# The start of a feed-forward stage: two weight blocks interleaved, with their operands built in a written order

## The chip, the cores and the metric

The kernel runs on one core of a Trainium2 chip. The metric is the device time of one execution in microseconds (us), taken as the median of several executions. Its engines are TensorE (PE), VectorE (DVE), ScalarE (ACT), GpSimd (POOL) and SyncE (SP), whose queue issues most DMA transfers. Each engine takes its instructions in order.

## The reference

One layer of a decoder over 1040 positions of width 1024 (16 learned meta tokens and 1024 tokens), all in float32:

```python
u = rmsnorm(h, mix_norm)
proj = u @ w_in + b_in                      # attention, gated linear attention and gate inputs
mixed = sigmoid(gate_a) * (y_att @ w_proj_attn) + sigmoid(gate_b) * (y_gla @ w_proj_gla)
h = h + mixed @ w_out
u = rmsnorm(h, ffn_norm)
a, v = split(u @ w_up, 2)                   # 1024 x 5632; a and v are 2816 wide
h = h + (gelu(causal_dwconv3(a)) * v) @ w_down
return rmsnorm(h, final_norm)[:, 16:]
```

## The kernel before

Every float32 operand of a matmul is split into a high part, rounded for the fast matmul type (ScalarE, a cast), and a low part, the rest (VectorE, a subtraction); a product is then three matmuls, high by high, high by low and low by high (L949 to L951).

The stages follow each other: the input projection (names d_q, d_gk, d_g), attention and gated linear attention woven into the gate projections, the output projection `w_out` (d_wo), the feed-forward product with `w_up` (m) and with `w_down` (dn). The residual h is held transposed in `hT`: eight strips of 128 channels by two halves of the tokens, 514 columns each, the first two columns of the second half being a copy of the last two of the first.

The `w_up` product is done in 22 blocks of 256 output channels; even blocks give a, odd ones v. Each block uses the seven-product form of a 2 x 2 matrix product: A11 to A22 are quarters of the weights (128 output channels by four strips), B11 to B22 quarters of u (four strips by one half of the tokens). P1, P2, P3 and P4 use B11, B21, B22 and T4; P5, P6, P7 use T1, T2, T3. The T operands are sums of quarters of u, made once, and all eight operands stay in SBUF as high and low parts. The weight sums S1 to S4 are made for each block on GpSimd (`sum_make`), and `w_split` splits the weight quarter of a product into one of six tiles. A product of an even block is two groups of 12 matmuls (258 and 256 columns), one of an odd block 12 matmuls of 512.

Around the change, from the last strips of `w_out` to the third block: `wout` adds a strip of the output projection to `hT` and squares it, with the squares summed on GpSimd into `rs`; `norm2` turns these sums into 1/rms by a matmul with `ones_m`, a square root and a reciprocal over all columns; `turn_out` transposes one half of `hT` on TensorE and stores it to DRAM for the final residual; `u2` scales a strip by its gain and 1/rms; `op_split` makes the high and low part of an operand. For the second half of the tokens all this comes after the last strip of `w_out`. Of the sums for the T operands, T1 (L1076) and T2 (L1081) are subtracted on VectorE, T3 (L1080) and T4 (L1089) on GpSimd.

The order of the instructions on each engine isn't that of the text: a planner in the framework reorders them by estimated costs and by the order of the text where two are ready. Buffers of a pool with the same tag follow each other in one place, and a new one waits for the last use of the old. PSUM has eight banks, named by the tags mm (3), s (2), pt (1) and pv (2).

In the input projection `tsum` loads pairs of `w_down` strips, sums them on VectorE and stores the sums to DRAM (`tw`, `t_d`); it is called once before every chunk of several products. The rotary step of the attention inputs goes through one buffer, `rs`, filled by four small transfers that ScalarE's queue issues (L314).

Of the kernel before, what the change touches and what calls it, by code (L numbers as in the profile page):

```python
# [46 lines left out]
def hybrid_block(ctx, tc, x, meta, mix_norm, w_in, b_in, w_alpha, b_alpha, sinks, ghn,  # L47
# [376 lines left out]
    run("gk0", CH_ALL, evac_gq(gk, bcol[:, 7:8], 1.0, 0), tsum)  # L424
# [439 lines left out]
    def turn_out(hf, tag, pool_):  # L864
        ht = pool_.tile([P, 4, D], F32, tag=tag, name=f"ht{hf}")
        for j in range(4):
            for h in range(2):
                tp = bank("pv" if h else "pt", f"th{hf}_{j}_{h}")
                for k in range(4):
                    pe.transpose(tp[:, k * P:k * P + P], hT[:, h * 4 + k, hf, 2 + j * P:2 + j * P + P], ident)  # L870
                (dve.tensor_copy if h else act.copy)(ht[:, j, h * 512:h * 512 + 512], tp)
# [24 lines left out]
    FIRST, ORDER = ("P1", "P2", "P3", "P6", "P7", "P5", "P4"), ("P1", "P2", "P6", "P7", "P5", "P3", "P4")  # L896
    seq = [(b, pn) for b in range(NB) for pn in (ORDER if b else FIRST)]
# [410 lines left out]
```

## Time and profile before

| | us |
|---|---|
| median of 3 runs (1442.51 to 1447.55) | 1442.79 |
| the profiled execution, its device time | 1442.23 |
| its span | 1440.5 |
| TensorE busy in the span | 1374.3 |
| VectorE busy | 913.5 |
| ScalarE busy | 581.6 |
| GpSimd busy | 426.0 |

A matmul's busy time includes an end that overlaps the next one, so a TensorE that is busy all the time may still be running at its lower clock. Idle time of an engine matters only where the next work of TensorE waits for it.

### The profile page before, as it was taken

Reading aid. Unit: us, or ns where it says so; the run is one execution under the profiler, and the core shown is the slowest. Engines: PE = TensorE matmul, PEld = TensorE weight load, DVE = VectorE, ACT = ScalarE, POOL = GpSimd, SP = SyncE. Lnnn points to the kernel's source line nnn. Section 1 sums busy time; section 2 is a strip of 40 time slices with the busy share of each in tenths; the row PEclk is TensorE's granted clock in tenths of the full one; section 3 lists DMA queues with packets and bytes.
Section 4 is the critical chain, followed back from the end, with each engine's and each line's share of the span. In section 5 each row is a group of like instructions: output and inputs, shape, how many; then the busy total and the mean of one; then the engine's idle time right before and its main releaser. Section 6 shows DMA issues by size and latency. Waiting matters only on the chain.

```text
span 1440.5 us, 21775 instructions
## 1 busy us (share of the span) xinstructions
PE 1374.3 (95%) x8213; PEld 1247.5 (87%) x8213; DVE 913.5 (63%) x1478; ACT 581.6 (40%) x1143; POOL 426.0 (30%) x298
## 2 busy tenths in 40 slices
PE   6979999989999999999996899999999999999997
PEld 6979999878989989999875788999999888788886
DVE  6565212566778876443659877776667777665674
ACT  6313221544545555443443433333323333554452
POOL 0220110111122222223234465676567653100000
PEclk9999999999999999999997999999999999999999
DMA  7789711113222324554321133332332234976642
GB/s 216 220 256 308 234 49 51 59 51 75 80 77 73 82 74 138 173 156 132 132 88 58 45 103 103 111 109 82 110 110 87 83 110 175 354 261 195 194 152 117
DMA packets 160871, 190.23 MB, mean 132 GB/s; under 512 B 19082, under 2 KB 115142, under 8 KB 160758
## 3 DMA queue, kind: packets, MB, share of 16 engines
q1 hardware_dynamic: 157670, 180.25, 39.7%
q10 hardware_dynamic: 3088, 8.51, 1.9%
q8 instruction: 67, 1.10, 0.3%
q14 instruction: 46, 0.38, 0.1%
HBM read 133.33 MB, written 52.74 MB: 129 GB/s over the span
## 4 chain that ended last, share of the span: by engine, by line
PE 68%; DVE 7%; ACT 1%; issue 1%; DMA 1%; POOL 1%; SPq 0%; DVEq 0%; ACTq 0%; POOLq 0%
PE m L951 10%; PE m L949 10%; PE m L950 10%; PE dn L1233 5%; PE dn L1234 5%; PE dn L1232 5%; PE d_g L91 3%; PE d_g L92 3%; PE d_g L93 3%; PE d_wo L91 2%; PE d_wo L92 2%; PE d_wo L93 2%; PE d_pj L91 2%; PE d_pj L92 2%; PE d_pj L93 2%
## 5 line engine op out<-in xcount | busy, mean ns | idle before, releaser
L949 PE MATMUL m<-op_T,wq 128*128 128x258 f32 (+2 forms) x528 | 170.8, 326 | 8.3 <-ACT op_T L889 8.3
L950 PE MATMUL m<-op_T,wq 128*128 128x258 f32 (+2 forms) x528 | 171.0, 324 | 1.3 <-DVE op_T L890 1.1
L951 PE MATMUL m<-op_T,wq 128*128 128x258 f32 (+2 forms) x528 | 170.1, 323 | 1.3 <-DVE wq L938 1.3
L91 PE MATMUL d_g<-uh,hi_g 128*128 128x342 f32 x480 | 159.6, 332 | 2.5 <-PEq L568 2.4
L92 PE MATMUL d_g<-ul,hi_g 128*128 128x342 f32 x480 | 157.0, 327 | 3.0 <-issue 3.0
L93 PE MATMUL d_g<-uh,lo_g 128*128 128x342 f32 x480 | 157.0, 327 | 0.0
L951 PE MATMUL m<-op_B,wq 128*128 128x256 f32 (+2 forms) x396 | 127.3, 322 | 4.4 <-DVE wq L938 4.4
L949 PE MATMUL m<-op_B,wq 128*128 128x256 f32 (+2 forms) x396 | 127.6, 323 | 1.6 <-ACT op_B L889 1.2
L950 PE MATMUL m<-op_B,wq 128*128 128x256 f32 (+2 forms) x396 | 127.6, 322 | 1.1 <-DVE op_B L890 1.1
L937 ACT CAST wq<-S 128x512 fp32r<-128x512 f32 x88 | 54.4, 623 | 170.7 <-PE m L951 154.6
L949 PEld LDWEIGHTS m<-op_T,wq 128*128 128x128 f32 x528 | 101.4, 193 | 16.8 <-ACT op_T L889 8.8
L950 PEld LDWEIGHTS m<-op_T,wq 128*128 128x128 f32 x528 | 101.5, 192 | 10.3 <-DVE op_T L890 2.4
L951 PEld LDWEIGHTS m<-op_T,wq 128*128 128x128 f32 x528 | 101.5, 193 | 9.2 <-DVE wq L938 1.5
L91 PEld LDWEIGHTS d_g<-uh,hi_g 128*128 128x128 f32 x480 | 93.1, 194 | 6.5 <-ACT gev L398 3.0
L93 PEld LDWEIGHTS d_g<-uh,lo_g 128*128 128x128 f32 x480 | 93.0, 194 | 3.8 <-issue 3.6
L938 DVE TENSOR_TENSOR wq<-st,wq 128x512 fp32r<-128x512 f32 x66 | 77.2, 1171 | 28.1 <-ACT wq L937 28.1
L92 PEld LDWEIGHTS d_g<-ul,hi_g 128*128 128x128 f32 x480 | 93.2, 194 | 0.5 <-issue 0.4
L965 DVE TENSOR_TENSOR wk<-wk,m 128x512 f32<-128x512 f32 (+2 forms) x99 | 55.1, 566 | 49.4 <-PE m L951 48.2
L1019 POOL TENSOR_TENSOR wk<-wk 128x1024 f32<-128x1024 f32 x22 | 58.1, 2643 | 93.1 <-DVE wk L965 90.7
L951 PEld LDWEIGHTS m<-op_B,wq 128*128 128x128 f32 x396 | 75.3, 190 | 10.6 <-DVE wq L938 4.8
L950 PEld LDWEIGHTS m<-op_B,wq 128*128 128x128 f32 x396 | 75.2, 190 | 7.7 <-DVE op_B L890 1.9
L949 PEld LDWEIGHTS m<-op_B,wq 128*128 128x128 f32 x396 | 75.0, 190 | 7.8 <-ACT op_B L889 1.4
(312 smaller groups left out, 3702.2 us busy)
## 6 DMA issues: line engine op xcount, KB each, us to landing
st<-in_w_up_dram SPq DMA_DIRECT2D x22, 1024.0 KB, 7.1
stage<-g_d SPq DMA_DIRECT2D x77, 256.0 KB, 4.5
tw<-in_w_down_dram SPq DMA_DIRECT2D x11, 1024.0 KB, 8.8
t_d<-tw SPq DMA_DIRECT2D x11, 1024.0 KB, 5.2
stage<-t_d SPq DMA_DIRECT2D x44, 256.0 KB, 3.0
gate_d<-gev SPq DMA_DIRECT2D x60, 171.0 KB, 2.9
st_g<-in_w_in_dram SPq DMA_DIRECT2D x20, 512.0 KB, 4.8
g_d<-wk SPq DMA_DIRECT2D x11, 768.0 KB
```

Source lines behind the costliest of these rows:

```text
L91: pe.matmul(o[:, :n], hi[:, k, :], rh(k), start=(k == 0), stop=False)
L92: pe.matmul(o[:, :n], hi[:, k, :], rl(k), start=False, stop=False)
L93: pe.matmul(o[:, :n], lo[:, k, :], rh(k), start=False, stop=(k == nk - 1))
L938: dve.tensor_tensor(t[:, 1], src, f32(t[:, 0]), ALU.subtract)
L949: pe.matmul(o[:, :m], t[:, 0, k], bh[:, k, a:a + m], start=(k == 0), stop=False)
L950: pe.matmul(o[:, :m], t[:, 0, k], bl[:, k, a:a + m], start=False, stop=False)
L951: pe.matmul(o[:, :m], t[:, 1, k], bh[:, k, a:a + m], start=False, stop=(k == 3))
L965: dve.tensor_tensor(dv[:, w], sv[:, w], o[:, :m], ALU.add)
L1019: pool.tensor_tensor(v, v, wk[:, 1028 + f * 1024:2052 + f * 1024].rearrange("p (h n) -> p h n", h=2), ALU.mult)
L1232: pe.matmul(o, gh[:, ts], dh, start=first, stop=False)
L1233: pe.matmul(o, gh[:, ts], dl, start=False, stop=False)
L1234: pe.matmul(o, gl[:, ts], dh, start=False, stop=last_)
```

## The change

The first two blocks of the `w_up` product are interleaved, and the stretch from the seventh strip of `w_out` to the last product of the second block is put in the order of the text on TensorE, VectorE, ScalarE and GpSimd (`manual_schedule`); SP's queue is still planned. In detail:

- Both first weight blocks are loaded early into one tile (`st01`), and their sums S1 and S3, S2 and S4 are made on GpSimd partly during `w_out`, in place of the quarters (`sum_first`). P1 and P2 of both blocks come first, then P3, P5, P6, P7, P4 of the two in turn.
- The second half of the tokens is transposed strip by strip (`turn_strip`), six of the eight strips during `w_out`, with all copies out of PSUM on ScalarE.
- The 1/rms of the second half is made token-major: eight matmuls of one column give the mean squares with tokens on partitions, root and reciprocal are taken over four columns, and four diagonal matrices (`dg`) times ones spread the result over a PSUM bank (`bc`), which `u2` reads.
- All eight sums for the T operands are on VectorE, in pairs of strips (1028 columns).
- The scratch tile `wk` is no longer a tile of its own but the place of `hT`. The gating of the first pair of blocks is moved into the third block.
- One product of the input projection, gk0, no longer calls `tsum` (three calls); the calls that are left come three chunks later.

```diff
-    run("gk0", CH_ALL, evac_gq(gk, bcol[:, 7:8], 1.0, 0), tsum)
+    run("gk0", CH_ALL, evac_gq(gk, bcol[:, 7:8], 1.0, 0))
...
+    def turn_strip(ht, k, tag="pv"):
+        tp = bank(tag, f"th1_{k}")
+        for j in range(4):
+            pe.transpose(tp[:, j * P:j * P + P], hT[:, k, 1, 2 + j * P:2 + j * P + P], ident)
+        act.copy(ht[:, :, k * P:k * P + P], tp.rearrange("p (j n) -> p j n", j=4))
+        if k % 4 == 3:
+            c = k // 4 * 512
+            sp.dma_start(h_d[4:8, :, c:c + 512].rearrange("j p n -> p j n"), ht[:, :, c:c + 512])
...
-    def u2(k, hf):
-        hv = hT[:, k, hf]
-        dve.scalar_tensor_tensor(hv, hv, fcol[:, k:k + 1], rs[hf], ALU.mult, ALU.mult)
-
-    def op_split(nm, i, m, src, eng=None):
-        hv, lv = (t[:, i:i + m] for t in ops[nm])
-        act.copy(hv, src)
-        (eng or dve).tensor_tensor(lv, src, f32(hv), ALU.subtract)
+    def u2(k, hf, scale=None):
+        hv = hT[:, k, hf, 2 if hf else 0:]
+        dve.scalar_tensor_tensor(hv, hv, fcol[:, k:k + 1], scale if hf else rs[hf], ALU.mult, ALU.mult)
+    def op_hi(nm, i, m, src):
+        act.copy(ops[nm][0][:, i:i + m], src)
+    def op_lo(nm, i, m, src):
+        dve.tensor_tensor(ops[nm][1][:, i:i + m], src, f32(ops[nm][0][:, i:i + m]), ALU.subtract)
...
-    FIRST, ORDER = ("P1", "P2", "P3", "P6", "P7", "P5", "P4"), ("P1", "P2", "P6", "P7", "P5", "P3", "P4")
-    seq = [(b, pn) for b in range(NB) for pn in (ORDER if b else FIRST)]
+    FIRST, ORDER = ("P3", "P5", "P6", "P7", "P4"), ("P1", "P2", "P6", "P7", "P5", "P3", "P4")
+    seq = [(b, pn) for b in range(2) for pn in ("P1", "P2")] + [(b, pn) for pn in FIRST for b in range(2)]
+    seq += [(b, pn) for b in range(2, NB) for pn in ORDER]
...
+    EARLY = ["s", "mm", "pv", "mm", "s", "mm", "pv", "s", "mm", "mm", "pt", "s", "mm", "pv", "mm", "s", "pv", "pv",
+             "mm", "pt", "mm"]
     def next_bank(name):
+        if EARLY:
+            return bank(EARLY.pop(0), name)
...
+    def sum_first(b, half):
+        a11, a12, a21, a22 = (quarter(b, q) for q in ("A11", "A12", "A21", "A22"))
+        s1 = s1t[:, b]
+        if half == 0:
+            pool.tensor_tensor(s1, a21, a22, ALU.add)
+            pool.tensor_tensor(a21, a11, a21, ALU.subtract)
+        else:
+            pool.tensor_tensor(a11, s1, a11, ALU.subtract)
+            pool.tensor_tensor(a12, a12, a11, ALU.subtract)
+        sums[b] = {"S1": s1, "S2": a11, "S3": a21, "S4": a12}
...
+            if mid and out_:
+                mid()
...
+    st01 = big.tile([P, 2, KT, 2, P], F32, tag="B1", name="st01")
+    s1t = p2.tile([P, 2, 4, P], F32, tag="xt", bufs=1, name="s1t")
+    hts = []
+    for i in range(6):
         wout(i, take(f"wo{i}_1"), (2,))
         if i == 0:
             norm2(0)
             norm2(1)
         elif i == 1:
-            turn_out(0, "B0", big)
-            pool.tensor_copy(hT[:, :, 1, 0:2], hT[:, :, 0, HQ - 2:HQ])
-            pool.tensor_copy(rs[1][:, 0:2], rs[0][:, HQ - 2:HQ])
+            hts.append(big.tile([P, 4, D], F32, tag="B0", name="ht0"))
+            turn_out(hts[0])
             op_tile(("B11", "B21"), big, "A")
             st_load(0)
-        elif i < 6:
+            st_load(1)
...
+                op_hi(nm, k % 4, 1, hT[:, k:k + 1, 0])
+                op_lo(nm, k % 4, 1, hT[:, k:k + 1, 0])
+            if i > 2:
+                if i == 3:
+                    hts.append(big.tile([P, 4, D], F32, tag="B0", name="ht1"))
+                for k in ((0, 1), (2, 3), (4,))[i - 3]:
+                    turn_strip(hts[1], k)
+            if i > 3:
+                sum_first(i - 4, 0)
+    pool.tensor_copy(hT[:, :, 1, 0:2], hT[:, :, 0, HQ - 2:HQ])
+    with tc.manual_schedule(engines={mybir.EngineType.PE, mybir.EngineType.DVE, mybir.EngineType.Activation,
+                                     mybir.EngineType.Pool}):
+        wout(6, take("wo6_1"), (2,))
+        turn_strip(hts[1], 5)
+        w_split(0)
+        w_split(3)
+        w_last = take("wo7_1")
+        w_split(1)
+        w_split(2)
+        o = dense(w_last, lambda k: mh[k // 4][:, k % 4, 514:1026], lambda k: ml[k // 4][:, k % 4, 514:1026], KT, 512,
+                  "wo7_2")
+        turn_strip(hts[1], 6)
+        hv = hT[:, 7, 1, 2:]
+        dve.tensor_tensor(hv, hv, o, ALU.add)
+        sq = p2.tile([P, 512], F32, tag="sg0", bufs=2, name="sq_last")
+        act.activation(sq, hv, AF.Square)
+        for b in range(2):
+            sum_first(b, 1)
+        op_tile(("B22",), big, "C1")
+        op_tile(("T2",), big, "C2")
+        op_tile(("T1",), b2, "E")
+        w_split(4)
+        w_split(5)
+        pr = {0: product(0)}
+        nt = bank("pt", "nt")
+        for j in range(4):
+            pe.matmul(nt[:, j:j + 1], rs[1][:, 2 + j * P:2 + j * P + P], ones_m[:, 0:1], start=True, stop=False)
+            pe.matmul(nt[:, j:j + 1], sq[:, j * P:j * P + P], ones_m[:, 0:1], start=False, stop=True)
+        act.activation(rt4[:, 0], nt[:, 0:4], AF.Sqrt, bias=eps_c, scale=1.0)
+        dve.reciprocal(rt4[:, 1], rt4[:, 0])
+        dg = p2.tile([P, 4, P], F32, tag="sg1", bufs=2, name="dg")
+        for j in range(4):
+            if j % 2:
+                dve.tensor_scalar(dg[:, j], ident, rt4[:, 1, j:j + 1], None, ALU.mult)
+            else:
+                act.activation(dg[:, j], ident, AF.Identity, scale=rt4[:, 1, j:j + 1])
+        bc = bank("pt", "bc")
+        turn_strip(hts[1], 7)
+        def spread():
+            for j in range(4):
+                pe.matmul(bc[:, j * P:j * P + P], ones_f, dg[:, j], start=True, stop=True)
+        pr[1] = product(1, spread)
+        p1a = b2.tile([P, HQ], F32, tag="rs1", name="p1_0")
+        p1v = b2.tile([P, HQ], F32, tag="rs0", name="p1_1")
+        keep_prod(0, p1a, pr[0])
+        w_split(6)
+        pr[2] = product(2)
+        w_split(7)
+        p2.release()
+        fp = tc.alloc_tile_pool(name="fp", bufs=1, reuse_waits="tile")
+        aa0 = fp.tile([P, 2, HQ], F32, name="aa0")
+        vt = fp.tile([P, 4, 4, P], F32, tag="S", bufs=1, name="vt").rearrange("p a k n -> p (a k n)")
+        vt = vt[:, 0:1024].rearrange("p (a n) -> p a n", a=2)
+        st_load(2)
+        st_load(3)
+        keep_prod(1, p1v, pr[2])
+        pr[3] = product(3)
+        def lo22(k):
+            op_lo("B22", k - 4, 1, hT[:, k:k + 1, 1])
+        for k in range(4, 8):
+            u2(k, 1, bc)
+            op_hi("B22", k - 4, 1, hT[:, k:k + 1, 1])
+            if k > 4:
+                lo22(k - 1)
+        lo22(7)
+        pr[4] = product(4)
+        pr[5] = product(5)
+        wk = hT.rearrange("p k h n -> p (k h n)")
+        def madd(dst, src, prod, off):
+            for o, a, m in prod:
+                dve.tensor_tensor(dst[:, a - off:a - off + m], src[:, a - off:a - off + m], o[:, :m], ALU.add)
+        def half(k, hf):
+            return hT[:, k:k + 2, hf]
+        madd(aa0[:, 0], p1a, pr[1], 0)
+        for k in range(4):
+            u2(k, 1, bc)
+        for k in (0, 2):
+            dve.tensor_tensor(half(k, 0), half(k, 1), half(k, 0), ALU.subtract)
+            op_hi("T1", k, 2, half(k, 0))
+        w_split(8)
+        for k in (0, 2):
+            op_lo("T1", k, 2, half(k, 0))
+        madd(vt[:, 0], p1v, pr[3], 2)
+        pr[6] = product(6)
+        pr[7] = product(7)
+        keep_prod(0, aa0[:, 1], pr[4])
+        keep_prod(1, vt[:, 1], pr[5])
+        for k in (0, 2):
+            dve.tensor_tensor(half(k, 1), half(k + 4, 1), half(k, 1), ALU.subtract)
+        op_tile(("T3",), big, "B0")
+        for k in (0, 2):
+            dve.tensor_tensor(half(k + 4, 1), half(k + 4, 1), half(k, 0), ALU.subtract)
+            op_hi("T2", k, 2, half(k + 4, 1))
+        w_split(9)
+        for k in (0, 2):
+            op_lo("T2", k, 2, half(k + 4, 1))
+            op_hi("T3", k, 2, half(k, 1))
+        pr[8] = product(8)
+        pr[9] = product(9)
+        w_split(10)
+        w_split(11)
+        for k in (0, 2):
+            op_lo("T3", k, 2, half(k, 1))
+        w_split(12)
+        w_split(13)
+        op_tile(("T4",), big, "B1")
+        for k in (0, 2):
+            dve.tensor_tensor(half(k + 4, 0), half(k + 4, 0), half(k + 4, 1), ALU.subtract)
+            op_hi("T4", k, 2, half(k + 4, 0))
+        madd(p1a, p1a, pr[8], 0)
+        madd(p1v, p1v, pr[9], 2)
+        for k in (0, 2):
+            op_lo("T4", k, 2, half(k + 4, 0))
+        pr[10] = product(10)
+        pr[11] = product(11)
+        pr[12] = product(12)
+        ca, cv, cv0 = whole(0, 1), whole(1, 1), whole(1, 0)
+        act.copy(cv0[:, 0], vt[:, 0])
+        w_split(14)
+        madd(ca[:, 0], p1a, pr[10], 0)
+        madd(ca[:, 1], ca[:, 0], pr[6], 0)
+        madd(aa0[:, 1], aa0[:, 1], pr[6], 0)
+        w_split(15)
+        pr[13] = product(13)
+        madd(cv[:, 0], p1v, pr[11], 2)
+        madd(cv[:, 1], cv[:, 0], pr[7], 2)
+        madd(cv0[:, 1], vt[:, 1], pr[7], 2)
+        sum_make(2)
+        dve.tensor_tensor(aa0[:, 1], aa0[:, 1], p1a, ALU.add)
+        w_split(16)
+        conv(0, 0)
+        madd(ca[:, 0], ca[:, 0], pr[12], 0)
+        conv(0, 1)
+        w_split(17)
+        dve.tensor_tensor(cv0[:, 1], cv0[:, 1], p1v[:, 0:512], ALU.add)
+        madd(cv[:, 0], cv[:, 0], pr[13], 2)
...
-    for n in range(2, len(seq)):
+    for n in range(14, len(seq)):
...
-            if pn == ("P5" if b == 0 else "P3"):
+            if b == 2 and pos in (2, 3):
+                gated(0, pos - 2)
+            if pn == "P3":
...
-    tl = b2.tile([P, 7, D], F32, tag="H", name="tl")
+    tl = wk[:, 0:7 * D].rearrange("p (a n) -> p a n", a=7)
```

## Rows read from the trace of the kernel before

**Rows 1.** Page: busy us, share of the span, instructions of an engine.
```profile
PE 1374.3 (95%) x8213; PEld 1247.5 (87%) x8213; DVE 913.5 (63%) x1478; ACT 581.6 (40%) x1143; POOL 426.0 (30%) x298
```

**Rows 2.** Waits of TensorE: line, released by, us in total, times, longest.
```profile
PE m L949 <- ACT op_T L889: 8.3, 2, 5.4
PE d_gk L91 <- ACT rt L308: 7.4, 1, 7.4
PE m L951 <- DVE wq L938: 5.7, 2, 4.4
```

**Rows 3.** Windows: length; busy PE, PEld, DVE, ACT, POOL; granted clock; DMA share; GB/s.
```profile
744.60:821.00 76.40, 55.28 (x288) 46.41 (x287) 67.47 (x83) 31.52 (x51) 33.14 (x22) 0.82 0.20 69
821.00:861.00 40.00, 40.00 (x256) 36.29 (x255) 29.45 (x41) 14.29 (x22) 26.85 (x15) 1.00 0.30 99
```

**Rows 4.** Timeline of TensorE: start, length, line, operation, count, idle before.
```profile
707.14 2.25 PE L870 MATMUL th<-ident,hT 128*128 128x128 f32 x16
...
744.60 0.28 PE L949 MATMUL m<-op_B,wq 128*128 128x258 f32 x1
...
747.51 1.12 PE L858 MATMUL n<-rs,ones_m 128*128 128x512 f32 x2
...
820.91 0.28 PE L949 MATMUL m<-op_B,wq 128*128 128x258 f32 x1
...
860.65 0.28 PE L949 MATMUL m<-op_B,wq 128*128 128x258 f32 x1
```

**Rows 5.** Timeline of VectorE in the same stretch.
```profile
753.39 3.34 DVE L860 RECIPROCAL rs<-rs 128x512 f32<-128x512 f32 x1
...
766.27 2.07 DVE L885 SCALAR_TENSOR_TENSOR hT<-hT,ccol,rs 128x514 f32<-128x514 f32 x3
768.26 2.49 DVE L1076 TENSOR_TENSOR hT<-hT 128x514 f32<-128x514 f32 x4
771.92 5.16 DVE L1081 TENSOR_TENSOR hT<-hT 128x514 f32<-128x514 f32 x3 [1.16 <-POOL hT L1080]
...
789.67 0.74 DVE L965 TENSOR_TENSOR aa<-p,m 128x258 f32<-128x258 f32 x2
790.49 6.03 DVE L890 TENSOR_TENSOR op_T<-hT,op_T 128x514 fp32r<-128x514 f32 x4
```

**Rows 6.** Timeline of GpSimd beside them.
```profile
769.09 7.44 POOL L1080 TENSOR_TENSOR hT<-hT 128x514 f32<-128x514 f32 x4 [16.16 <-DVE hT L1076]
...
789.38 1.53 POOL L923 TENSOR_TENSOR S<-st 128x512 f32<-128x512 f32 x1 [5.61 <-DVE wq L938]
```

**Rows 7.** VectorE and GpSimd on 1026 columns, in the input projection.
```profile
82.30 1.22 DVE L73 TENSOR_TENSOR lo_gk<-st_gk,hi_gk 128x1024 fp32r<-128x1024 f32 x1
83.43 1.22 DVE L327 TENSOR_TENSOR c<-rt,rs 128x1026 f32<-128x1026 f32 x1
...
106.61 3.44 DVE L316 TENSOR_TENSOR rt<-rt,cs 128x1026 f32<-128x1026 f32 x1
...
106.53 2.42 POOL L315 TENSOR_TENSOR rs<-rs,sn 128x1026 f32<-128x1026 f32 x1 [7.63 <-DMA rs<-rt]
```

**Rows 8.** Timeline of ScalarE: casts of 514 columns; its queue's transfers.
```profile
777.11 2.19 ACT L889 CAST op_T<-hT 128x514 fp32r<-128x514 f32 x4 [0.58 <-DVE hT L1081]
...
84.73 3.99 ACTq L314 DMA_DIRECT2D rs<-rt  x4
```

**Rows 9.** Windows of two us around stalls of TensorE (columns as in rows 3).
```profile
84.00:86.00 2.00, 0.00 (x0) 0.00 (x0) 1.97 (x4) 0.00 (x0) 0.00 (x0) 0.82 0.59 154
...
92.00:94.00 2.00, 2.00 (x16) 2.00 (x16) 0.00 (x0) 0.13 (x1) 0.00 (x0) 0.97 1.02 329
...
766.00:768.00 2.00, 0.88 (x6) 0.54 (x4) 2.00 (x4) 0.62 (x1) 0.00 (x0) 0.99 0.00 0
...
784.00:786.00 2.00, 2.00 (x13) 1.72 (x13) 2.00 (x4) 0.00 (x0) 0.00 (x0) 0.74 0.00 0
```

**Rows 10.** Window of the input projection after its stall (columns as in rows 3).
```profile
100.00:120.00 20.00, 20.00 (x127) 20.00 (x127) 15.78 (x18) 4.53 (x8) 2.63 (x2) 1.00 0.94 291
```

More of the change, by code (lines that the diff above doesn't have):

```diff
@@ L169, in hybrid_block @@
     ones_r = cp.tile([P, 1], F32, name="ones_r")
+    ones_f = cp.tile([P, P], F32, name="ones_f")
+    rt4 = cp.tile([P, 2, 4], F32, name="rt4")
     def mask_make():
@@ L173, in mask_make @@
         pool.memset(ones_r, 1.0)
+        pool.memset(ones_f, 1.0)
         for t, sh, cm, st, base in ((mkf, [P, P], -1, 1, 0), (mkt, [P, P], 1, -1, 0), (m0f, [2, NM], 1, -1, QS)):
@@ L796, in hybrid_block @@
     ml0 = b2.tile([P, 4, NQ], F32R, tag="E", name="ml0")
-    rs = [b2.tile([P, HQ], F32, name=f"rs{h}") for h in range(2)]
+    rs = [b2.tile([P, HQ], F32, tag=f"rs{h}", name=f"rs{h}") for h in range(2)]
     p2 = tc.alloc_tile_pool(name="p2", bufs=1)
@@ L907, in st_load @@
     def st_load(b):
-        if b == 0:
-            t = big.tile([P, KT, 2, P], F32, tag="B1", name="st0")
+        if b < 2:
+            t = st01[:, b]
         else:
@@ L939, in w_split, with product @@
         slots[n] = t
-    def product(n):
+    def product(n, mid=None):
         b, pn = seq[n]
@@ L967, in hybrid_block, with keep_prod @@
     C11, C12, C21, C22 = (0, 0), (0, 1), (1, 0), (1, 1)
+    def keep_prod(b, dst, prod):
+        for o, a, m in prod:
+            a -= b % 2 * 2
+            act.copy(dst[:, a:a + m], o[:, :m])
     def combine(b, pn, prod):
@@ L972, in combine @@
             sb["p1"] = fp.tile([P, HQ], F32, tag="p1", bufs=1, name=f"p1_{b}")
-            for o, a, m in prod:
-                a -= b % 2 * 2
-                act.copy(sb["p1"][:, a:a + m], o[:, :m])
+            keep_prod(b, sb["p1"], prod)
         elif pn == "P2":
@@ L1033, in hybrid_block @@
         wout(i, take(f"wo{i}_0"), (0, 1))
-    for i in range(KT):
+    st01 = big.tile([P, 2, KT, 2, P], F32, tag="B1", name="st01")
+    s1t = p2.tile([P, 2, 4, P], F32, tag="xt", bufs=1, name="s1t")
+    hts = []
+    for i in range(6):
         wout(i, take(f"wo{i}_1"), (2,))
@@ L1064, in hybrid_block @@
-    op_tile(("T2",), big, "C2")
-    op_tile(("T1",), big, "B0")
-    op_tile(("T3",), b2, "E")
-    w_split(2)
-    w_split(3)
-    for k in range(4, 8):
-        u2(k, 1)
-        op_split("B22", k - 4, 1, hT[:, k:k + 1, 1])
-    for k in range(4):
-        u2(k, 1)
-    for k in range(4):
-        b11, b12, b21, b22 = hT[:, k, 0], hT[:, k, 1], hT[:, k + 4, 0], hT[:, k + 4, 1]
-        dve.tensor_tensor(b11, b12, b11, ALU.subtract)
-        dve.tensor_tensor(b22, b22, b11, ALU.subtract) if False else None
@@ L1090, in hybrid_block @@
-    for k in range(4):
-        op_split("T4", k, 1, hT[:, k + 4:k + 5, 0])
-    wk = b2.tile([P, 8 * 2 * HQ], F32, tag="H", name="wk")
+                op_hi(nm, k % 4, 1, hT[:, k:k + 1, 0])
[7 more added lines that the diff above has]
+                sum_first(i - 4, 0)
```

56 lines of the change are left out of this document (10 added, 46 removed).

## The prediction

> **What bounds the kernel now.** I read the page first: TensorE is busy 95% of the span and VectorE 63%, so a gain has to come from the few places where TensorE waits or runs slow [rows 1]. The list of TensorE's waits has three entries of some weight: the first T operands (L949, 8.3 us in two waits), the start of gk0 (7.4 us) and a weight split in the first blocks (L951, 5.7 us) [rows 2]. Two of the three lie where the change is. The windows then show the size of that place: in the 76.4 us from 744.6 on, TensorE is busy 55.3 us at a mean granted clock of 0.82, while VectorE is busy 67.5; in the next window of 40 us TensorE is busy throughout at 1.00 and VectorE 29.5 [rows 3]. So up to the third block VectorE sets the pace, and from there on TensorE does.
>
> The timeline of TensorE gives the exact stretch. The first product starts at 744.60, the third block at 820.91, the fifth at 860.65 [rows 4]. Two blocks at full pace take 860.65 - 820.91 = 39.7 us, the first two take 76.3. To the 39.7 belong 32 transposes of the second half, twice the 2.25 us of sixteen, and the 1.1 us of the norm's matmul [rows 4]: 45.3 us of work. The other 31.0 us are idle time and half clock, and that is what can be had.
>
> Why VectorE is slow there: four subtractions on 514 columns take 2.49 us, 0.62 each, when GpSimd rests. From 769.09 GpSimd makes the T3 sums, and the same kind takes 5.16 us for three, 1.72 each; while GpSimd makes weight sums from 789.38, the low parts take 6.03 us for four, 1.51 each [rows 5, 6]. An addition that reads PSUM, in the same stretch, keeps its pace (0.74 us for two of 258) [rows 5]. In the input projection 1026 columns take 1.13 us (start to start) alone and 3.44 beside GpSimd [rows 7]. A reciprocal over 512 columns takes another 3.34 us, and all of the second half's operands wait for it [rows 5].
>
> **The change part by part.** The stretch is now in written order, so I walk it, with t in us from the last matmul of w_out. Prices: a product 39.7/14 = 2.84; a strip of transposes 2.25/4 = 0.56; VectorE 0.62 on 514 columns, 1.13 on 1028, 0.69 for the scaling (2.07 for three), 0.37 to add 258 columns from PSUM, some 0.62 for 512; ScalarE 0.55 a cast of 514 (2.19 for four), 1.1 for 1028 [rows 4, 5, 7, 8]. No row shows a one-column matmul or the four spreading ones. Eight of the first cost between nothing and eight transposes, 1.1 us; the four, on 512 columns together, between nothing and the 1.1 us of the norm's matmul, which has as many columns. I take 1.1 for each, as both load weights each time.
>
> Strips: six of eight move into w_out, where TensorE is the bound: 3.4 us longer there. Their copies go to ScalarE, which is busy 40% of the span [rows 1], so they are hidden; without that cover they cost 0.55 each. Then TensorE: strip, P1, eight columns, strip, P2 with the spreading inside, P1 and P2 of block 1: t = 0.6, 3.4, 4.5, 5.1, 9.0, 11.9, 14.7. All of it has its weights: GpSimd's four sums S2 and S4, at some 1.5 us each [rows 6], finish near t = 3, before VectorE's small reciprocal is due. They stand ahead of it in VectorE's queue through two weight splits, at no cost unless they end past t = 4.5.
>
> P3 needs B22. VectorE reaches the scaling only after the weight split for the seventh product, whose tile comes free when P2 ends: 9.0 + 0.55 + 0.62, with handing over 10.4. Two scalings later ScalarE still holds the copy of block 1's P1 (t = 11.9) ahead of the first cast, so the last low part is ready at 17.1: TensorE loses 1.5 us, and both P3 end at 21.9.
>
> P5 needs T1. VectorE: two additions, four scalings, two subtractions, to 22.8; ScalarE casts until 23.9; then a weight split stands ahead of the low parts on both engines (24.6, 25.2), and the first low part of T1 is there at 26.4. TensorE waits 4.5 us, and 0.5 for the second: 5.0. Both P5 end at 32.6. P6 needs T2: after T1, one addition and the subtractions for T3 and T2 take VectorE to 32.7, casts and the next weight split to 35.1, the low part to 36.2: TensorE waits 4.2 us. P7 finds T3 ready, P4 waits 1.2 us for a PSUM bank that VectorE empties. Work 39.7 + 1.1 + 1.1 + 1.1 = 43.0, waits 1.5 + 5.0 + 4.2 + 1.2 = 11.9: the third block starts at t = 54.9. With the 3.4 us of the strips that is 58.3 against 76.3, a gain of 18.0.
>
> So VectorE decides three of the four waits in the walk. The sums that move to it, T3 and T4, cost it 4 x 1.13 = 4.5 us. What goes is the blocked time, 5.16 - 3 x 0.62 = 3.3 us on three T2 sums, 6.03 - 4 x 0.62 = 3.6 on the four low parts shown and more on others like them, and the reciprocal's 3.3. The scalings now read `bc` in PSUM. An addition that reads PSUM takes 0.37 us on 258 columns against 0.62 on 514 in SBUF [rows 5], so I charge nothing for it. By the Trainium skill's page "Perfetto Trace Analysis", section "Optimizing Scalar/DVE Operations", a VectorE instruction pays about 60 ns to reach SBUF and 125 ns PSUM; the eight scalings would be 0.5 us dearer in all by this estimate; no row here shows a scaling from PSUM.
>
> The clock: around the wait before 768 it falls from 0.99 to half, and is back in the window at 784; around the wait at 82 it falls at 84 and is back by 92 [rows 9]. After the 5.0 us wait the P5 would run at half clock for some us, but VectorE, which makes T2 meanwhile, isn't slowed, so what TensorE loses comes off its wait of 4.2. After that it costs 0 to 5 us: 17 us at half clock, as from 768 to 785, lose 8.5, less the 3.7 that are then left of the second wait. I take 0.5, since the walk feeds TensorE without a break from there on.
>
> Transfers: both first weight loads stand ahead of w_out's strips on SP's queue, one MB more, 3.6 us at the 291 GB/s of a busy window [rows 10]; strips are loaded ahead, so 0 to 3.6, I take 0. The store of the last four strips and the loads of blocks 2 and 3, three MB or 11 us behind it on that queue, are done near t = 18; T3 takes the store's buffer at 33, the third block's weights are split at 46. Fixed order also moves the first gating (two products of 1024 columns and four sums on GpSimd) into block 2, where GpSimd is otherwise busy 26.9 of 40 us [rows 3]: hidden, or up to 3 if two weight sums of 1.5 us queue behind it.
>
> gk0 without `tsum`: the wait of 7.4 us has ScalarE's rotary transfers (issued at 84.73 for 3.99 us) behind the rotary buffer [rows 2, 8]. The loads of `tsum` share the transfer engines, but they run as soon as their two buffers are free, far ahead of the text, so I expect the same transfers at the same time: 0. The other end is the whole wait and what half clock loses from its end, near 89.3, to 92: 7.4 + 1.3 = 8.7 [rows 2, 9].
>
> Sum: 1442.2 (the profiled execution, 1.7 outside its span) - 18.0 + 0.5 = 1424.7; the median of the runs is 0.6 above that execution, so **1425 us**.
>
> **The rivals.** *gk0's wait goes too:* 1425 - 8.7 = 1416. For it: fewer transfers beside the rotary ones. Against: the loads are free to run early, and from 100 to 120 the transfer engines are 0.94 busy with TensorE at full pace [rows 10], so an earlier start may meet them. Chance 0.18.
>
> *A new wait takes part of the gain:* half clock (up to 5), late weight strips (3.6) or the gating ahead of block 3's sums (3), two of them together: 1431 to 1437. For it: before, the clock stayed low for 17 us [rows 9]. Against: there TensorE was fed piecemeal all the time. Chance 0.14.
>
> *VectorE stays slow (the other side):* if its sixteen subtractions on 1028 columns for the T operands ran at the 3.44 us that they take beside GpSimd and not at 1.13 [rows 7], each costs 2.3: eight of them eat the gain, from eleven on the kernel is over 0.5% slower, all sixteen give 1425 + 37 = 1462. For it: VectorE is the stage's bound, and now has more to do. The Trainium skill's page "Perfetto Trace Analysis" (section named above) says to hand work away from a saturated VectorE, to GpSimd if need be, and the change does the opposite. Against: GpSimd has no instruction between its S4 and the sums of the third block. Chance 0.05 slower, 0.05 near no change.
>
> **How the numbers follow.** Likeliest case 0.58 (1419 to 1431). The range takes in the first rival and the short end of the second: **1414 to 1434**; outside stay some 0.2. Half a per cent, 7 us, is about what a measurement of this kernel can tell from no change. Faster by more: 0.58 + 0.18 + 0.09 of the second = 0.85; within: 0.05 of the second + 0.05 = 0.10; slower: 0.05.
>
> **What would show it.** In the changed profile, the third block should start some 55 us after the last w_out matmul; subtractions on 1028 columns should read near 1.2 us, none beside a busy GpSimd; TensorE's waits should be on the low parts of T1 and T2, 4 to 5 us each; gk0's wait should be unchanged. The prediction is wrong if TensorE waits ahead of P1, if the clock stays at half past the P6, or if w_out itself gets gaps.

## The result

The changed kernel takes **1422.75 us** in the median of four runs (1421.07 to 1429.04), the kernel before 1444.63 us beside it (1442.51 to 1447.55): ratio 0.9855, 95% interval 0.9818 to 0.9892. The forecast was 1425 us, range 1414 to 1434. The profiled execution of the changed kernel took 1421.07 us, its span is 1419.3 us.

The page of the changed kernel, first part, answers to [rows 1]:

```profile
PE 1368.4 (96%) x8235; PEld 1244.9 (88%) x8235; DVE 911.1 (64%) x1467; ACT 582.6 (41%) x1145; POOL 416.5 (29%) x289
```

Next the list of TensorE's waits in the changed kernel, beside [rows 2] (line, released by, us in total, times, longest):

```profile
PE d_gk L91 <- ACT rt L311: 8.4, 1, 8.4
PE m L979 <- DVE op_T L902: 5.5, 3, 3.1
...
PE m L978 <- ACT op_T L899: 0.8, 1, 0.8
...
PE m L979 <- DVE op_B L902: 0.6, 1, 0.6
```

The wait in front of gk0 is still there. The products' two entries of [rows 2], 14.0 us, and four smaller ones of the same list, 3.7 us together, have become three of 6.9 us.

The timeline of TensorE in the changed kernel shows where the stage now stands, beside [rows 4] (start, length, line, operation, count, idle before and its releaser):

```profile
747.36 0.60 PE L879 MATMUL th<-ident,hT 128*128 128x128 f32 x4
747.71 0.36 PE L978 MATMUL m<-op_B,wq 128*128 128x258 f32 x1
...
750.64 0.28 PE L1118 MATMUL nt<-ones_m,rs 128*128 128x1 f32 x2
...
752.35 0.63 PE L879 MATMUL th<-ident,hT 128*128 128x128 f32 x4
754.26 1.05 PE L1133 MATMUL bc<-dg,ones_f 128*128 128x128 f32 x8
...
763.99 0.38 PE L979 MATMUL m<-op_B,wq 128*128 128x258 f32 x1 [0.64 <-DVE op_B L902]
...
770.29 0.39 PE L978 MATMUL m<-op_T,wq 128*128 128x258 f32 x1 [0.80 <-ACT op_T L899]
773.81 0.39 PE L979 MATMUL m<-op_T,wq 128*128 128x258 f32 x1 [3.14 <-DVE op_T L902]
...
783.57 0.38 PE L979 MATMUL m<-op_T,wq 128*128 128x258 f32 x1 [2.21 <-DVE op_T L902]
...
841.98 0.28 PE L978 MATMUL m<-op_B,wq 128*128 128x258 f32 x1
```

The first product starts 3.1 us later than before (747.71 against 744.60). From w_out's first matmul to it are 99.4 us, before 96.5: 2.9 us more, since seven strips of transposes now run there. The fifth block starts at 841.98 against 860.65, 18.7 us earlier [rows 4]. I take the fifth block as the mark and not the third: the third block's P1 now runs ahead of the last P4s.

One window over that whole stretch, from the first product to the fifth block, first of the kernel before, then of the changed one (length; TensorE busy; granted clock; DMA share; GB/s):

```profile
744.60:860.65 116.05, 94.94 (x540) 0.88 0.24 80
```

```profile
747.71:841.98 94.27, 87.19 (x535) 0.96 0.23 74
```

The stretch is 21.8 us shorter. Idle time fell from 21.1 to 7.1 us (14.0), busy time by 7.75 us; the mean clock rose from 0.88 to 0.96. Less the 3.1 us of the later start that is the 18.7. The other 2.5 us of the span's 21.2 lie in the down-projection, 219.5 us from its first matmul to the end against 222.0: the clock in the 40 us around its start was 0.96 before and is 1.00 now. That part wasn't forecast. 0.7 us of it lie behind the last matmul (7.5 us in the kernel before and in e9, 6.8 in every changed one). The rest goes with the clock's fall to half there in the kernel before, and such a fall comes and goes: e9 below has none, and e7, with the whole change, has one and takes 223.1 us.

VectorE in the changed kernel, beside [rows 5]:

```profile
753.04 0.17 DVE L1121 RECIPROCAL rt<-rt 128x4 f32<-128x4 f32 x1
...
755.51 0.69 DVE L965 TENSOR_TENSOR wq<-s1t,wq 128x512 fp32r<-128x512 f32 x1 [1.78 <-ACT wq L964]
757.49 0.69 DVE L965 TENSOR_TENSOR wq<-s1t,wq 128x512 fp32r<-128x512 f32 x1 [1.29 <-ACT wq L964]
758.10 1.40 DVE L896 SCALAR_TENSOR_TENSOR hT<-hT,ccol,bc 128x512 f32<-128x512 f32 x2
...
765.29 2.72 DVE L896 SCALAR_TENSOR_TENSOR hT<-hT,ccol,bc 128x512 f32<-128x512 f32 x4
767.92 2.36 DVE L1177 TENSOR_TENSOR hT<-hT 128x1028 f32<-128x1028 f32 x2
771.92 0.69 DVE L965 TENSOR_TENSOR wq<-st,wq 128x512 fp32r<-128x512 f32 x1 [1.63 <-ACT wq L964]
772.53 2.36 DVE L902 TENSOR_TENSOR op_T<-hT,op_T 128x1028 fp32r<-128x1028 f32 x2
```

Two subtractions on 1028 columns take 2.36 us, and no pair up to 800 us takes longer. But VectorE still idles in front of weight splits (L965) that stand ahead of the operand work: the spread root was complete near 755.3 us, and the scaling (L896) began at 758.10; the cast of T1's first half was done near 770.3, its low part (L902) began at 772.53.

### The profile page after: what moved, and what is told of

It is laid out like the page before. It is cut to its first block, busy times and chain, and to the rows that moved or that the text cites. A ratio compares the mean times of both kernels' runs of the same rounds, so it can differ in the third digit from the quotient of the medians.

```text
span 1419.3 us, 21786 instructions
## 1 busy us (share of the span) xinstructions
PE 1368.4 (96%) x8235; PEld 1244.9 (88%) x8235; DVE 911.1 (64%) x1467; ACT 582.6 (41%) x1145; POOL 416.5 (29%) x289
## 4 chain that ended last, share of the span: by engine, by line
PE 69%; DVE 5%; DMA 2%; ACT 2%; issue 1%; SPq 0%; DVEq 0%; ACTq 0%
PE m L979 10%; PE m L978 10%; PE m L980 10%; PE dn L1376 5%; PE dn L1377 5%; PE dn L1375 5%; PE d_g L91 3%; PE d_g L92 3%; PE d_g L93 3%; PE d_wo L91 2%; PE d_wo L93 2%; PE d_wo L92 2%; PE d_pj L91 2%; PE d_pj L92 2%; PE d_pj L93 2%
## 5 line engine op out<-in xcount | busy, mean ns | idle before, releaser
L964 ACT CAST wq<-S 128x512 fp32r<-128x512 f32 x80 | 49.4, 622 | 148.7 <-PE m L980 127.2
L965 DVE TENSOR_TENSOR wq<-st,wq 128x512 fp32r<-128x512 f32 x72 | 84.8, 1183 | 28.9 <-ACT wq L964 28.9
L1046 POOL TENSOR_TENSOR hT<-hT 128x1024 f32<-128x1024 f32 x22 | 58.8, 2674 | 84.4 <-DVE hT L994 81.9
L965 DVE TENSOR_TENSOR wq<-S,wq 128x512 fp32r<-128x512 f32 x80 | 68.0, 851 | 11.9 <-ACT wq L964 11.2
```

Source lines behind the costliest of these rows:

```text
L964: act.copy(t[:, 0], src)
L965: dve.tensor_tensor(t[:, 1], src, f32(t[:, 0]), ALU.subtract)
L1046: pool.tensor_tensor(v, v, wk[:, 1028 + f * 1024:2052 + f * 1024].rearrange("p (h n) -> p h n", h=2), ALU.mult)
```

## The experiments

**My theory** after this: the gain is cover. The second block's products run while VectorE makes the first block's next operand, and TensorE's higher clock follows from fewer long waits. **Rivals:** VectorE's shorter operations alone give it; the written order gives it; the narrow root gives it. A second question is what holds the 7.1 us that are left: work that stands ahead of the operands on an in-order VectorE, or VectorE's total work.

All runs in one table. Ratios are against the kernel before on the same chip. "Stretch" goes from the first product to the fifth block, with TensorE's idle time and mean granted clock in it, from one window of each profile.

| Kernel | Median us | Ratio (95%) | Stretch | Idle | Clock |
|---|---|---|---|---|---|
| before | 1444.63 | | 116.05 | 21.1 | 0.88 |
| changed | 1422.75 | 0.9855 (0.9818-0.9892) | 94.27 | 7.1 | 0.96 |
| e1 serial | 1441.11 | 0.9956 (0.9935-0.9978) | 110.69 | 17.2 | 0.89 |
| e2 sums on GpSimd | 1426.86 | 0.9856 (0.9838-0.9875) | 95.31 | 8.6 | 0.95 |
| e3 planner's order | 1418.52 | 0.9796 (0.9775-0.9816) | 88.62 | 4.2 | 1.00 |
| e4 wide root | 1420.52 | 0.9821 (0.9797-0.9845) | 92.99 | 7.1 | 0.96 |
| e5 B22 first | 1423.48 | 0.9854 (0.9825-0.9883) | 91.24 | 5.4 | 0.96 |
| e6 T low parts first | 1421.36 | 0.9821 (0.9789-0.9853) | 91.62 | 4.9 | 0.98 |
| e7 both first | 1418.50 | 0.9820 (0.9798-0.9841) | 88.91 | 4.7 | 1.00 |
| e8 T3 before T2 | 1416.03 | 0.9808 (0.9784-0.9831) | 89.49 | 4.2 | 0.98 |
| e9 before, sums on VectorE | 1442.53 | 0.9970 (0.9954-0.9987) | 112.62 | 16.8 | 0.89 |
| e10 gk0's loads back | 1419.78 (one run) | | 94.01 | 7.1 | 0.96 |
| e11 e8 in planner's order | 1418.59 | 0.9807 (0.9764-0.9850) | 88.54 | 4.1 | 1.00 |
| e12 e11 with wide root | 1422.03 | 0.9837 (0.9810-0.9865) | 89.38 | 5.3 | 1.00 |

The runs of one kernel lie up to 13 us apart (e6: 1414.38 to 1427.36), and the kernel before had a median of 1444.63 to 1447.69 us on the chips used, so differences of a few us are read from the stretch. Its length repeats: e10 has the changed kernel's stage, unchanged, and reads 94.01 against 94.27. From the fifth block to the first matmul of the down-projection all fourteen profiles take 357.8 us, so what the stretch gains isn't lost behind it.

### e1: the interleaving undone

```
-seq = [(b, pn) for b in range(2) for pn in ("P1", "P2")]
-    + [(b, pn) for pn in FIRST for b in range(2)] ...
+seq = [(b, pn) for b in range(2) for pn in ("P1", "P2") + FIRST] ...
```

with weight splits, PSUM banks and the second block's sums placed to match; the second block's weights are loaded later.

> The changed kernel with the interleaving undone: all seven products of the first block, then all seven of the second; sums, root, strips and the written order stay (the second block's weights come later, as in the kernel before). Theory A (the gain is cover: the second block's products fill TensorE while VectorE makes the next operand): the first block's products then wait for B22, T1, T2, T3 and T4 one after the other, its P4 ends near 797 us, and the second block's seven products of 2.8 us (19.6 us) come behind it, so that the third block starts some 16 to 18 us later: 1437 to 1443 us. Theory B (VectorE's shorter operations alone give the gain, the order of the products is a matter of taste): within 5 us of the changed kernel's 1422.75, at most 1428 us.

Theory A. The stretch is 16.4 us longer than the changed kernel's, and the clock is back at 0.89. The window and TensorE's waits of this run:

```profile
748.41:859.10 110.69, 93.49 (x535) 0.89 0.23 74
```

```profile
PE m L979 <- DVE op_T L902: 10.3, 5, 3.1
...
PE m L978 <- ACT op_T L899: 4.0, 3, 2.4
...
PE m L979 <- DVE op_B L902: 1.6, 3, 0.6
PE m L978 <- ACT op_B L899: 1.2, 1, 1.2
```

The first block waits for every operand in turn; its P4 ends at 799.8 us (forecast 797), and the second block's seven products follow without a gap until 819.34, 19.6 us. The sums on VectorE, the small root and the strips were all in place and left 5.4 us of the stretch's 21.8, and 2.9 of these only moved into w_out.

Not all of the 16.4 us is cover. The second block's weights come later here, so GpSimd makes its sums, and the third block's, from 780 to 795 us, beside VectorE's operand work:

```profile
787.00 4.53 DVE L1193 TENSOR_TENSOR hT<-hT 128x1028 f32<-128x1028 f32 x2
...
792.11 3.85 DVE L902 TENSOR_TENSOR op_T<-hT,op_T 128x1028 fp32r<-128x1028 f32 x2
```

```profile
785.95 2.27 POOL L941 TENSOR_TENSOR S<-st 128x512 f32<-128x512 f32 x1
```

T2's and T3's low parts, T4's sums and T4's low parts take 3.44, 3.44, 4.53 and 3.85 us where the changed kernel takes 2.36 each, 5.8 us more in all. TensorE's waits behind them (0.56 us at T2; 0.87, 2.91 and 0.56 at T4) add up to 4.9 us. So up to 4.9 us of the 16.4, and the half clock behind these waits, can be GpSimd's; a serial order with the sums made early was not run.

### e2 and e9: the sums' engine

```
-dve.tensor_tensor(half(k, 1), half(k + 4, 1), half(k, 1), ALU.subtract)       # T3
+pool.tensor_tensor(half(k, 1), half(k + 4, 1), half(k, 1), ALU.subtract)
-dve.tensor_tensor(half(k + 4, 0), half(k + 4, 0), half(k + 4, 1), ALU.subtract)  # T4
+pool.tensor_tensor(half(k + 4, 0), half(k + 4, 0), half(k + 4, 1), ALU.subtract)
```

> The changed kernel with the sums of T3 and of T4 on GpSimd again, at the same places of the written order. Theory A (the sums' engine matters because T2's sum waits for T3's and because GpSimd is slow beside VectorE): two T3 sums take some 3.7 us each (the row of before has 1.86 us for half the columns) in place of 1.18, T2's low parts are 5 us later, TensorE's wait for T2 grows from 2.4 to about 7 us with a longer stretch at half clock; T4's are late by less than its cover: 1427 to 1431 us. Theory B (off the path, hidden behind the products): within 1 us of 1422.75.

Close to theory B, by another way than either said: the stretch is 1.0 us longer than the changed kernel's. The median is 4.1 us above that kernel's, but it was taken on another chip, and the ratios agree. VectorE and GpSimd in this run:

```profile
772.54 4.54 DVE L902 TENSOR_TENSOR op_T<-hT,op_T 128x1028 fp32r<-128x1028 f32 x2
...
777.60 2.36 DVE L1191 TENSOR_TENSOR hT<-hT 128x1028 f32<-128x1028 f32 x2
...
782.30 4.17 DVE L902 TENSOR_TENSOR op_T<-hT,op_T 128x1028 fp32r<-128x1028 f32 x2
```

```profile
768.81 6.03 POOL L1188 TENSOR_TENSOR hT<-hT 128x1028 f32<-128x1028 f32 x2 [17.54 <-DVE hT L1177]
778.89 5.36 POOL L1207 TENSOR_TENSOR hT<-hT 128x1028 f32<-128x1028 f32 x2 [4.04 <-DVE hT L1191]
```

GpSimd starts T3 early, beside T1's low parts, which then take 4.54 us in place of 2.36, and TensorE's longest wait for T1 grows from 3.1 to 5.8 us. But VectorE is spared T3's 2.36 us, and the wait for T2 falls from 2.2 to 1.0. Moving the sums swaps blocked time for work, nearly one for one. T3's sums and T1's low parts overlap for 2.3 us (772.54 to 774.84), and the low parts take 2.2 us longer. That a subtraction of two SBUF operands stands still while GpSimd works is as the Trainium skill's page "SBUF — State Buffer", section "SBUF: two separate sides", has it (an exclusive lock on a shared pair of ports).

The other side of the same question, in the kernel before:

```
-pool.tensor_tensor(b12, b22, b12, ALU.subtract)
+dve.tensor_tensor(b12, b22, b12, ALU.subtract)
-pool.tensor_tensor(hT[:, k + 4, 0], hT[:, k + 4, 0], hT[:, k + 4, 1], ALU.subtract)
+dve.tensor_tensor(hT[:, k + 4, 0], hT[:, k + 4, 0], hT[:, k + 4, 1], ALU.subtract)
```

> The kernel before with one part of the change alone: its sums of T3 and T4 on VectorE in place of GpSimd. Theory A (the gain is cover from the second block's products; the sums' engine is worth little, as in the run that put them back): the third block starts 0 to 4 us earlier, 1440 to 1445 us. Theory B (VectorE slowed by GpSimd is the larger loss of the kernel before): 8 us or more faster, under 1437 us.

Theory A: 3.4 us in the stretch, ratio 0.9970. VectorE of this run, beside [rows 5]:

```profile
776.93 1.28 DVE L1081 TENSOR_TENSOR hT<-hT 128x514 f32<-128x514 f32 x2
...
792.19 6.06 DVE L890 TENSOR_TENSOR op_T<-hT,op_T 128x514 fp32r<-128x514 f32 x4
```

T2's sums are at full pace, but the low parts beside GpSimd's weight sums (L923 to L929, from 791 us on) still take 6.06 us for four, as before [rows 5, 6].

### e3: the written order taken away

```
-    with tc.manual_schedule(engines={PE, DVE, Activation, Pool}):
+    if True:
```

> The changed kernel without the order written out: same program text, the order within each engine left to the planner as in the rest of the kernel. Theory A (the written order does part of the work, since a planner that sorts by its own costs moves operand work behind weight splits or products): 3 to 12 us slower, 1426 to 1435 us, seen in longer waits of TensorE between 757 and 800 us. Theory B (the parts do it, whichever order): within 2 us of 1422.75.

Neither theory: the planner's order is *better*, by 5.7 us in the stretch, ratio 0.9796. Its window and its VectorE and ScalarE at T1:

```profile
750.75:839.37 88.62, 84.47 (x536) 1.00 0.22 73
```

```profile
769.87 0.68 DVE L965 TENSOR_TENSOR wq<-st,wq 128x512 fp32r<-128x512 f32 x1
770.47 2.36 DVE L902 TENSOR_TENSOR op_T<-hT,op_T 128x1028 fp32r<-128x1028 f32 x2
```

```profile
768.60 0.62 ACT L964 CAST wq<-st 128x512 fp32r<-128x512 f32 x1
769.12 2.01 ACT L899 CAST op_T<-hT 128x1028 fp32r<-128x1028 f32 x2
```

ScalarE casts the weights *before* T1's operand here, so that VectorE does the weights' low part while the operand is cast, and doesn't idle there. In the changed kernel the weight cast stands behind both operand casts, and VectorE idles 1.63 us for it. e7 below, which moves such work by hand, gains nearly as much.

### e4: the old form of the root

```
-8 x pe.matmul(nt[:, j:j+1], ..., ones_m[:, 0:1]); sqrt, reciprocal of 128x4; diagonal; spread
+pe.matmul(bcp, ones_m, rs[1][:, 2:HQ]); pe.matmul(bcp, ones_m, sq)
+act.activation(bc, bcp, AF.Sqrt, ...); dve.reciprocal(bc, bc)        # 128x512
```

(the pool that holds `aa0` and the next weights is opened behind the scaling, since the wide root lies in its place)

> The changed kernel with the old form of the root: two matmuls against the 128x128 matrix of ones (512 columns each) in place of the eight column matmuls, square root and reciprocal of 512 columns, no diagonal and no spreading. Theory A (the prediction's step: the root's 3.3 us on VectorE stands ahead of all operands): scaling starts 2 to 3.3 us later and the waits for B22 and T1 grow by it: 1424.5 to 1426.5 us. Theory B (in the changed kernel the scaling waits for two weight splits that stand ahead of it on VectorE, until 758.10 us, though the spread root was there at 755.07; the wide reciprocal would fit into that time): within 1 us of 1422.75.

Theory B: the wide root is no slower, the stretch is 1.3 us shorter. VectorE of this run:

```profile
749.86 3.35 DVE L1121 RECIPROCAL bc<-bc 128x512 f32<-128x512 f32 x1
753.13 1.22 DVE L965 TENSOR_TENSOR wq<-s1t,wq 128x512 fp32r<-128x512 f32 x2
754.27 1.41 DVE L896 SCALAR_TENSOR_TENSOR hT<-hT,ccol,bc 128x512 f32<-128x512 f32 x2
```

The 3.35 us fill time in which VectorE otherwise waits for weight casts: scaling starts 10.0 us after the first product (754.27 - 744.30), in the changed kernel 10.4 (758.10 - 747.71). TensorE's idle time is the same, 7.1 us; what the stretch loses is busy time.

### e5 to e8: operands ahead of weights

e5 moves the two weight splits for P5 and the copy of the second block's P1 behind B22; e6 moves one split each behind the low parts of T1 and T2; e7 does both; e8 also runs P7 before P6.

```
e5:  -w_split(6); ... w_split(7); ... keep_prod(1, p1v, pr[2])     before the scaling
     +w_split(6); w_split(7); keep_prod(1, p1v, pr[2])             after lo22(7)
e6:  -w_split(8)   before   op_lo("T1", ...)      +after it;  w_split(9) and T2 likewise
e8:  -FIRST = ("P3", "P5", "P6", "P7", "P4")
     +FIRST = ("P3", "P5", "P7", "P6", "P4")
     +madd(ca[:, 0], p1a, pr[8], 0); madd(tv, p1v, pr[9], 2)       # p1 + P7, P6 added later
```

> The changed kernel with two weight splits (for P5) and the copy of the second block's P1 moved behind the making of B22; nothing else. Theory A (VectorE works in order, and its idle 1.8 and 1.3 us at 753.9 to 757.5 in front of the scaling, with 1.2 us at 759.5, are waits of work that stands ahead of the operand): scaling starts near 755.3 instead of 758.10, no wait for B22 (0.9 before), T1's first low part 2.5 to 4 us earlier, so its waits of 3.9 us fall to about 1: 1417 to 1420 us. Theory B (the products' own work or the weights set the pace: what is moved back comes late for P5): within 1 us of 1422.75 or slower.

> The changed kernel with the weight split that stands between the casts and the low parts of T1, and the one at T2, moved behind those low parts; nothing else. Theory A (VectorE idles 1.63 and 1.64 us there for a weight cast that ScalarE does after both operand casts, then spends 0.6 us on it): T1's and T2's low parts come 2.2 us earlier, TensorE's waits of 3.1 and 2.4 us shrink by that each, the half-clock stretches behind them shrink too: 1416 to 1419 us. Theory B (the waits only move on to the next operand, since VectorE's total work sets the pace): T1 2.2 us shorter but T2 not, 1420 to 1422 us.

> Both moves, of B22 and of T1 and T2, together. Theory A (head of line on VectorE): TensorE's waits between 757 and 801 us fall from 7.2 us to 2.5 or less (what is left stands at T2, whose sum comes behind T3's), and the clock stays up in most of it: 1413 to 1417 us. Theory B (the pace is set by something else): no better than the better one of the two.

> Both moves, and in the first two blocks P7 (operand T3) runs before P6 (operand T2): T3's sum has to come before T2's in any case, so its operand is ready first; two more additions on VectorE (1.4 us) join the products. Theory A (the operand's readiness is all that TensorE waits for): no wait over 0.5 us after B22, 1411 to 1414 us. Theory B (PSUM banks held longer or VectorE's added work give a new wait at P6 or P4): 1414 to 1420 us.

The stretch is 3.0 us shorter in e5, 2.7 in e6 and 5.4 in e7, the sum of the two within 0.3. No theory A comes out whole. In e5 scaling starts 7.6 us after the first product (759.89 - 752.25) and no wait for B22 is left, as it had it, but the wait for T1 falls from 3.9 us only to 3.0, not to 1, for VectorE still idles 1.64 us there. In e6 the waits for T1 fall from 3.9 to 1.8 us, those for T2 only from 2.4 to 1.6, which is nearer theory B (the waits move on). In e7 theory B is out, since it beats both; each wait for T1 and T2 is 0.9 us or less and the clock is 1.00, but a new one of 1.6 us appears, for a PSUM bank that VectorE empties between T4's sums and low parts: 4.0 us together, where theory A had 2.5 or less. By their medians e5 and e6 can't be told from the changed kernel; their profiles already stood 4.5 and 8.8 us behind its profile when w_out ended, where nothing was changed (last section).

e8 misses its theory A in the stretch, which is 0.6 us longer than e7's. TensorE's waits of e8:

```profile
PE m L979 <- DVE op_T L902: 2.8, 4, 1.3
...
PE m L978 <- DVE hT L1168: 1.4, 1, 1.4
```

The wait of 1.3 us stands in the first P7: T3's second low part is late, since T2's sums stand ahead of it on VectorE. A bank for a product of the third block is late by 1.4. Theory B had waits of this kind, though at P6 or P4, and its time. The median, 1416.03 us, is the lowest of all, its interval (0.9784 to 0.9831) overlaps that of e3 and e7.

### e10 to e12

e10 only calls `tsum` under gk0 again (`run("gk0", ..., tsum)`). e11 is e8 without the written order; e12 is e11 with the wide root.

> The changed kernel with the loads of the down-projection's sums under gk0 again; one look, for the wait in front of gk0 alone. Theory A (the loads run when their buffers are free, whichever text position they have): the wait is 6.3 to 9.2 us, as in the ten profiles so far. Theory B (the loads held gk0 up): over 10 us, or under 5.

Theory A: the wait is 6.9 us. In the other profiles it is 6.3 to 9.2 us, with and without the loads.

> The kernel with both moves and P7 before P6, now without the order written out. Theory A (with every engine free to take what is ready, and T3 in front of T2, no wait over 1 us is left): from the first product to the fifth block 85 to 88 us, no half clock, 1412 to 1417 us. Theory B (the planner alone gave the gain of its run; the swap adds two additions on VectorE and holds PSUM banks longer): 88.5 us or more in that stretch, 1417 to 1421 us.

> The same with the old form of the root (wide reciprocal, two matmuls of 512 columns). Theory A (TensorE's eight column matmuls and four spreading ones cost it more than two wide ones, and the wide reciprocal is hidden): 1 to 1.5 us shorter in that stretch than the run before, as under the written order. Theory B (no weight split stands ahead of the scaling now, so the reciprocal's 3.3 us come into the path): 1 to 3 us longer, seen as a wait at P3.

Theory B for e11: 88.54 us, the same as e3; the swap adds nothing under the planner. For e12 theory B in kind: 0.8 us longer, just under its range, and the wait grows at T1 (0.3 to 1.1 us), not at P3. So the wide root seems to cost a little once no weight split stands ahead of the scaling, by one profile of each.

## Why the prediction was right, and where its terms were off

The forecast held, but its errors cancelled, which was luck. Its walk, counted from w_out's last matmul, put the fifth block at 54.9 + 39.7 = 94.6 us; measured are 94.6 (841.98 - 747.36). Its mark, the third block at t = 55, was missed in the letter: that block's P1 starts at 798.19, t = 50.8, ahead of the last P4s. Most of the 2.5 us in the down-projection is luck too.

**Operands: right.** Scaling was forecast at t = 10.4 and came at 10.7; T1's first low part at 26.4, and it was done near 773.7, t = 26.4; T2's at 36.2, done near 783.5, t = 36.1. Walking VectorE in order, with casts and weight splits in the queue, gave these. The waits for T1 (5.0 forecast) came out at 3.9 and for T2 (4.2) at 2.4, because TensorE reached them later; the wait for B22 was 0.6 to 0.9 in place of 1.5, and the bank wait of 1.2 didn't come. Idle in all: 7.1 against 11.9, too high by 4.8.

**TensorE's work: mis-sized.** The forecast has 94.0 us from the first product, so 82.1 of work. In e3 and e7, at clock 1.00, nearly the same matmuls take 84.5 and 84.2: 2 us more. The eight column matmuls took 1.7 us (750.64 to 752.35), not 1.1; the spreading took 0.8, not 1.1; a strip 0.4, not 0.56: together 0.1 more. The rest lies in the 28 products, 81.3 us in e7 (84.17 less 1.71, 0.81 and 0.39), 2.90 each, where I used 2.84, the mean of two blocks without a wait. The first product, behind transposes, takes 2.93 (747.71 to 750.64). Another part is at waits: a matmul of 258 columns there counts with its whole 0.28 us, and not with the 0.12 to the next one's start.

**The clock: mis-sized.** I took 0.5 us. Windows of the changed kernel around the two waits (columns as above):

```profile
763.71:773.71 10.00, 5.73 (x30) 1.00 0.14 43
773.71:777.71 4.00, 3.90 (x19) 0.57 0.01 4
777.71:783.71 6.00, 3.79 (x20) 1.00 0.00 0
783.71:787.71 4.00, 3.85 (x20) 0.60 0.00 0
```

The clock falls to half (1.2 of 2.4 GHz) twice, behind each wait, and is back within 4 us. Busy time is 87.2 us against 84.2 to 84.5 at full clock, so some 2.9 us went there. The first half of it should have come off the wait for T2, as the prediction argued, since VectorE wasn't slowed; the second was the loss that I had nearly left out.

**Why it is faster: the step was right in the sum, wrong in the shares.** The prediction gave the gain to blocked VectorE time (3.3 + 3.6 us and more) and to the reciprocal (3.3 us). e9 shows 3.4 us for the sums in the kernel before, e2 1.0 us in the changed one, and e4 shows that the reciprocal there costs nothing. What carries the gain is the interleaving, with the early weight sums that go with it: 16.4 us of 21.8 in e1, 10.1 of idle time (17.2 against 7.1) and 6.3 of busy time, with the clock at 0.89 against 0.96. Up to 4.9 us of that idle time stand behind work that GpSimd slowed. The walk had this in it, since it ran the second block's products beside VectorE, but the prediction named the wrong part. How much of the gain is blocked time, how much cover, no run here divides cleanly.

**Small terms.** gk0 at 0: right (e10). Scaling from PSUM at no extra: right, 0.68 us each (2.72 for four) against 0.69 from SBUF [rows 5]. The 0.5 us estimated by the Trainium skill's page "Perfetto Trace Analysis", section "Optimizing Scalar/DVE Operations", isn't seen. The strips cost 2.9 us ahead of the first product against the 4.0 forecast (3.4 + 0.6). Rival "VectorE stays slow": its pairs of subtractions are at 2.36 us throughout, since GpSimd stood idle from 752 to 800 us. The Trainium skill's page "Perfetto Trace Analysis", named for this rival, adds in the same section that GpSimd and VectorE share an SBUF read port, so that work moved between the two might not gain; e2's stretch, 1.0 us longer, agrees. Late weights and gating: no wait of TensorE in the stretch names them.

**What stays open.** Which of e3, e7, e8 and e11 is fastest can't be said from these runs. All have 4 to 5 us of idle time left, in waits of 1.6 us and less for an operand, a PSUM bank or a weight split, and over 84 us of work.

## What to carry to other kernels

When an engine makes operands in steps and TensorE waits after each, look first for independent products to put between; here moving the sums gave 1.0 and 3.4 us, and the cover, with the early weight sums that go with it, 16, of which 5 or a little more may be GpSimd's. A hand-written order can hold an operand up behind work that isn't urgent: look for idle time of the operand engine in front of work that nobody needs yet, and try the planner's order before keeping one's own. A faster operation gains nothing while something else ahead of the operand is late (e4), and may begin to matter when that is gone (e12, 0.8 us).

## What the runs showed of the hardware

Ahead of w_out TensorE runs the same 3863 matmuls of the trace in the same order in all profiles, yet w_out's first matmul starts between 644.8 us (e4) and 657.1 us (e6). The difference comes with the granted clock. Three windows of 40 us of e8 (w_out at 646.8 us) and of e7 (656.2 us), in the recurrent part of the kernel:

```profile
240.00:280.00 40.00, 39.48 (x230) 0.96 0.16 52
280.00:320.00 40.00, 33.16 (x230) 0.96 0.22 63
320.00:360.00 40.00, 38.65 (x257) 0.96 0.29 73
```

```profile
240.00:280.00 40.00, 40.00 (x214) 0.87 0.11 36
280.00:320.00 40.00, 33.22 (x225) 0.91 0.24 69
320.00:360.00 40.00, 38.67 (x233) 0.87 0.28 73
```

The same work falls to half clock for longer in one execution than in the other. If TensorE sets the pace, the three windows lose 4.8 us in e8 and 14.0 in e7. All of the time to 640 us, read in windows of 80 us, loses 12.8 and 24.8 by the same estimate, 12.0 more; w_out starts 9.4 later, so some of the lost clock must fall where TensorE waits anyway. Why the clock falls more often in one execution stays open. So a median of four runs moves by some us without any change of the code, and the stretch in the trace told apart what the medians couldn't.
